# A two-layer hybrid encoder trunk: small products on all 128 rows of the TensorE array

## The chip, the cores and the metric

The kernel runs on one core of a Trainium2 chip. The core has five engines that run side by side, each through its own list of instructions in order: PE (TensorE, matrix products; the loading of its stationary operand has a row of its own, PEld), DVE (VectorE), ACT (ScalarE), POOL (GpSimd) and SP (SyncE, which here only issues DMAs). They meet through semaphores. PE reads SBUF and writes PSUM; DVE and ACT take its results from there. The metric is the device time of one execution in microseconds (us).

## The reference

528 tokens (16 meta tokens and a sequence of 512) of width 2048 pass two layers. The first has a convolution branch and a sparse attention branch, the second a gated linear recurrence of 16 heads. The parts that matter here:

```python
# layer 0, attention: scores of an indexer choose 128 keys for each query
dots = jnp.einsum('bqhd,bsd->bqhs', qi_b, ki)          # 16 heads of width 64, one set of keys
score = jnp.einsum('bqh,bqhs->bqs', wi_b, jax.nn.relu(dots))
score = jnp.where(admissible[None], score, NEG_INF)
_, idx = lax.top_k(score, topk)
...
p = jax.nn.softmax(logits, axis=-1)                    # 8 heads, bias by distance
return jnp.einsum('bhqk,bqkc->bqhc', p, c_sel)

# layer 1, one chunk of the recurrence
o_inter = jnp.einsum('bhtk,bhkv->bhtv', q_c * jnp.exp(b), state)
attn = jnp.einsum('bhtk,bhtsk,bhsk->bhts', q_c, jnp.exp(diff), k_c)
o_intra = jnp.einsum('bhts,bhsv->bhtv', attn, v_c)
state = jnp.exp(b_last)[..., None] * state \
        + jnp.einsum('bhsk,bhsv->bhkv', k_c * jnp.exp(b_last[:, :, None] - b), v_c)
```

Everything is float32. Around these stand the large projections (2048 to 2048 and wider), which are most of the arithmetic.

## The kernel before

Channels lie on the 128 partitions, tokens along the free dimension. Every large projection is cut into stripes of 128 output channels (`stripe`, L147). A stripe's weights come in two halves of 128x1024, each loaded by SP (L139), split by ACT into a rounded part `wh` (L143) and by DVE into the remainder `wl` (L144), with three buffers of each. PE then makes three products for each of 16 blocks of 128 input channels: L160 (`wh` by `xh`), L161 (`wh` by `xl`), L162 (`wl` by `xh`). These are the main products. A stripe over all 528 tokens has two sums of 264 columns, one over the 512 sequence tokens a single sum of 512. DVE evacuates the sums (L168).

The other products are side work. A scheduler sets the order on every engine while the program is built: work has a level (`band`), weights before evacuations, then side work, then the convolution on DVE (L415). The side products therefore stand among the main products of later stripes.

The first layer goes through the steps of `EVEN` (L46). `g` are stripes of the convolution branch, `s` those of the indexer, `k` the selection of keys on DVE (L389, L390), `h` an attention head, `n` a norm.

- `scores` (L356): one stripe gives two indexer heads, head A on partitions 0 to 63, head B on 64 to 127. Each head's queries are split into a rounded part and a remainder; the tile `qa` holds the rounded part on A's half and the remainder on the other half, which a DMA on POOL brings there (L367). The keys stand twice, on both halves, as `kih` (rounded) and `kil` (remainder). For each head and each of four query blocks PE makes a pair: L377, the whole tile by `kih`, on 128 rows of the array, and L378, the rounded queries by `kil`, on the 64 rows of that head. The fourth block is wider than 512 keys and has two pairs. ACT takes the relu (L380), DVE adds it to the score (L381).
- `attend` (L432): for each head and query block, POOL fetches the bias by DMA (L437) and adds the mask (L439), PE makes logits (L445), DVE and ACT the softmax, PE turns the probabilities (L463; L466 for the 16 meta keys) and multiplies them with the values (L470). The values `Vt` have five blocks of keys; block 0 is that of the 16 meta tokens, so the first product of each sum uses 16 rows. `Vt` has three buffers and is filled for two heads at a time (L334 to L344).

In the second layer `rec_head` (L639) makes the recurrence of one head out of small products. The state after the meta tokens is L751, a product on 16 rows; the later states are L754, and L757 and L758 make the output. `vt` (two buffers) holds the values, again with 16 meta tokens in block 0, and `kk` the turned keys, with those of the meta tokens in slot 3.

An f32 product such as L470 is run by PE as two MATMULs, so a line's count in the trace can be twice that of the code.

Of the kernel before, what the change touches and what calls it, by code (L numbers as in the profile page):

```python
# [10 lines left out]
F32 = mybir.dt.float32  # L11
F32R = mybir.dt.float32r
# [3 lines left out]
OP = mybir.AluOpType  # L16
# [54 lines left out]
def trunk_kernel(ctx: ExitStack, tc: tile.TileContext, x: bass.AP, w: bass.AP, wukv: bass.AP,  # L71
# [141 lines left out]
    def et(shape, dt, name, bufs):  # L213
        return epools[EROLE.get(name, "es")].tile(shape, dt, name=name, bufs=bufs)
# [50 lines left out]
    with band(SIDE):  # L265
        p = ps1()
        for t in range(NB):
            P.transpose(p[:, t * NM:(t + 1) * NM], kw[64:80, NM + 128 * t:NM + 128 * (t + 1)],
                        ident[64:80, 64:80])
        V.tensor_scalar(wiT.rearrange("p a b -> p (a b)"), p[:, :NB * NM], 1.0 / 32, None, op0=OP.mult)  # L270

        ki = et([128, T], F32, "gt", 3)
        G.dma_start(ki[:64], kw[:64])
        G.dma_start(ki[64:], kw[:64])
        kih, kil = split(epools["ei"], ki, 1.0, "kih", "kil", bufs=1)

# [40 lines left out]
    def keys_values(pr):  # L317
# [3 lines left out]
        for hh in range(2):  # L321
# [11 lines left out]
            Ks.append(Kh)  # L333
        Vs = [et([128, 5, 128], F32, "Vt", 3) for _ in range(2)]  # L334
        for i, (s0, ns) in enumerate(blocks):
            p = ps1()
# [19 lines left out]
    def scores(j):  # L356
# [6 lines left out]
        with band(EVAC):  # L363
            for q, hf, other in ((qa, lo, up), (qb, up, lo)):
                S.activation(q[hf], ps[0][0][hf], AF.Copy)
                V.tensor_tensor(ql[hf], ps[0][0][hf], q[hf].bitcast(F32), op=OP.subtract)
                G.dma_start(q[other], ql[hf])  # L367
        with band(SIDE):
            for t in range(NB):
                for hh in range(2):  # L370
                    h, W = 2 * j + hh, wk(t)
                    q, hf = ((qa, lo), (qb, up))[hh]
                    qs = slice(128 * t, 128 * (t + 1))
                    for s0, s1 in (((0, W),) if W <= 512 else ((0, HT), (HT, W))):
                        p = ps1()
                        se = max(s1, s0 + 256)
                        P.matmul(p[:, :se - s0], q[:, qs], kih[:, s0:se], start=True, stop=False)  # L377
                        P.matmul(p[:, :se - s0], q[hf, qs], kil[hf, s0:se], start=False, stop=True)  # L378
                        r = et([128, T], F32, "sq", 3)
# [52 lines left out]
    def attend(h, qh, gb, Kh, Vt):  # L432
# [24 lines left out]
        for t in range(NB):  # L457
# [4 lines left out]
            for j in range(t + 1):  # L462
                P.transpose(p[:, j * 128:(j + 1) * 128], L[:, NM + 128 * j:NM + 128 * (j + 1)], ident)  # L463
            S.activation(pt[:, 1:t + 2, :], p[:, :128 * (t + 1)], AF.Copy)
            p = ps1()
            P.transpose(p[:NM, :128], L[:, :NM], ident)  # L466
            S.activation(pt[:NM, 0, :], p[:NM, :128], AF.Copy)
            for j in range(t + 2):
                ns = blocks[j][1]
                P.matmul(o[:, 128 * t:128 * (t + 1)], Vt[:ns, j, :], pt[:ns, j, :],  # L470
                         start=j == 0, stop=j == t + 1)
# [167 lines left out]
    def rec_head(h, fz, q, v):  # L639
# [26 lines left out]
        S.activation(vt[:, 1:, :], p, AF.Copy, scale=1.0 / (KS * QS))  # L666
        p = ps1()
        P.transpose(p[:NM, :128], v[:, :NM], ident)
        S.activation(vt[:NM, 0, :], p[:NM, :128], AF.Copy, scale=1.0 / (KS * QS))
# [68 lines left out]
        for j in range(3):  # L738
            P.transpose(p[:, j * 128:(j + 1) * 128], kb[:, 128 * j:128 * (j + 1)], ident)
        P.transpose(p[:NM, 384:512], k[:, :NM], ident)  # L740
        kk = ht([128, 4, 128], F32, "kk", 2)
        S.activation(kk[:, :3, :], p[:, :384], AF.Copy, scale=KS * QS)
        S.activation(kk[:NM, 3, :], p[:NM, 384:512], AF.Copy, scale=KS * QS)
        o = pso()
        st = None
        for j in range(NB):
# [3 lines left out]
            if j == 0:  # L750
                P.matmul(p[:, :128], kk[:NM, 3, :], vt[:NM, 0, :], start=True, stop=True)  # L751
                V.tensor_copy(new, p[:, :128])
# [236 lines left out]
```

## Time and profile before

| | |
|---|---|
| median of 3 runs | 2024.43 us (2021.56 to 2024.53) |
| profiled execution | 2024.44 us |
| its span, first to last instruction | 2022.6 us |
| PE busy | 1995.4 us, 99% |
| PEld busy | 1814.4 us, 90% |
| DVE busy | 1298.9 us, 64% |
| ACT busy | 811.9 us, 40% |
| POOL busy | 88.8 us, 4% |
| chain that ended last | 95% PE |

The matmuls of PE are pipelined and their ends are modelled: one product's duration runs over into the next. The time that a product costs is the distance from its start to the start of the next. In the timeline a row gives the start and the length of one instruction, or of several alike in a row (x2, x6); the shape `64*128` means 64 rows by 128 columns of the array.

### The profile page before, as it was taken

To read this page: it belongs to the slowest core of one execution; us is meant where nothing else is said; L and a number is where in the kernel's file an instruction comes from. 1 tells how busy PE (TensorE), PEld (TensorE's weight loads), DVE (VectorE), ACT (ScalarE), POOL (GpSimd) and SP (SyncE) were. 2 spreads that over 40 slices of the span, in tenths; PEclk is the share of its full clock that TensorE was granted. 3 is DMA by queue.
4 is the path that set the end of the run, shared out by engine and by line. 5 is a ranking of instruction groups with operands and counts; after the bars stand their busy time and mean duration, and the time that the engine had idled before them with its cause. 6 is when DMAs were issued, how large, how long until landed. Compare 5 with 4: busy or idle time off the path is not lost.

```text
span 2022.6 us, 34969 instructions
## 1 busy us (share of the span) xinstructions
PE 1995.4 (99%) x14524; PEld 1814.4 (90%) x14524; DVE 1298.9 (64%) x2400; ACT 811.9 (40%) x1392; POOL 88.8 (4%) x121
## 2 busy tenths in 40 slices
PE   8999999999999999999999999999999999999997
PEld 7988779999999999999999999999999988888886
DVE  6588868997738545433577777777777773445334
ACT  5323343234343534322444555545555443224322
POOL 1000000011112100000000000000000000000000
PEclk9999999999999999999999999999999999999999
DMA  5422322233232233444222222222222222223333
GB/s 187 117 80 79 93 70 90 75 102 93 89 97 73 83 115 117 143 142 136 96 74 74 80 78 74 74 74 74 80 78 74 79 84 94 94 94 110 116 118 120
DMA packets 63279, 193.24 MB, mean 96 GB/s; under 512 B 7632, under 2 KB 12024, under 8 KB 63120
## 3 DMA queue, kind: packets, MB, share of 16 engines
q1 hardware_dynamic: 59168, 182.21, 28.0%
q0 software_dynamic: 3952, 8.80, 1.7%
q8 instruction: 114, 1.87, 0.4%
q14 instruction: 45, 0.37, 0.1%
HBM read 177.38 MB, written 11.22 MB: 93 GB/s over the span
## 4 chain that ended last, share of the span: by engine, by line
PE 95%; DVE 2%; ACT 1%; DMA 1%; issue 0%; SPq 0%; DVEq 0%; ACTq 0%
PE mps L162 27%; PE mps L161 27%; PE mps L160 27%; PE po L470 2%; PE s L378 1%; PE s L445 1%; PE s L377 1%; PE s L636 1%; PE s L635 1%; PE s L637 1%; PE po L758 1%; PE po L757 1%; PE s L341 1%; PE s L754 1%; PE s L330 1%; ACT xh L175 1%
## 5 line engine op out<-in xcount | busy, mean ns | idle before, releaser
L160 PE MATMUL mps<-xh,wh 128*128 128x264 f32 (+2 forms) x3728 | 1162.1, 312 | 10.0 <-ACT wh L143 3.3
L161 PE MATMUL mps<-xl,wh 128*128 128x264 f32 (+2 forms) x3728 | 1166.8, 313 | 2.1 <-DVE xl L176 2.0
L162 PE MATMUL mps<-xh,wl 128*128 128x264 f32 (+2 forms) x3728 | 1167.0, 313 | 1.7 <-DVE wl L144 1.5
L160 PEld LDWEIGHTS mps<-xh,wh 128*128 128x128 f32 (+1 forms) x3728 | 701.9, 188 | 52.5 <-ACT wh L143 4.0
L161 PEld LDWEIGHTS mps<-xl,wh 128*128 128x128 f32 (+1 forms) x3728 | 701.2, 188 | 47.1 <-DVE xl L176 4.5
L162 PEld LDWEIGHTS mps<-xh,wl 128*128 128x128 f32 (+1 forms) x3728 | 701.3, 188 | 43.5 <-DVE wl L144 2.8
L143 ACT ACTIVATE wh<-w 128x1024 fp32r<-128x1024 f32 (+1 forms) x293 | 310.2, 1059 | 675.6 <-PE mps L161 540.6
L144 DVE TENSOR_TENSOR wl<-w,wh 128x1024 fp32r<-128x1024 f32 (+1 forms) x293 | 361.1, 1233 | 249.7 <-ACT wh L143 247.6
L415 DVE SCALAR_TENSOR_TENSOR z<-u,vec,z 128x528 f32<-128x528 f32 x240 | 188.8, 796 | 2.8
L631 ACT ACTIVATE qhm<-q 128x256 f16<-128x256 f32 x128 | 52.1, 419 | 56.3 <-DVE q L732 44.2
L717 DVE COPY_PREDICATED A<-msk,s 128x256 f32<-128x256 uint8 x96 | 46.6, 485 | 28.3 <-PE s L637 27.7
L632 DVE SCALAR_TENSOR_TENSOR qlm<-q,qhm 128x256 f16<-128x256 f32 x128 | 53.1, 425 | 16.0 <-ACT qhm L631 16.0
L380 ACT ACTIVATE sq<-s 128x264 f32<-128x264 f32 (+3 forms) x80 | 31.3, 394 | 62.8 <-PE s L378 62.1
L168 DVE TENSOR_TENSOR gt<-mps,rstd 128x264 f32<-128x264 f32 x64 | 27.6, 431 | 39.3 <-PE mps L162 38.6
L381 DVE SCALAR_TENSOR_TENSOR mask<-sq,wiT,mask 128x264 f32<-128x264 f32 (+3 forms) x80 | 38.3, 494 | 22.3 <-ACT sq L380 21.9
L570 DVE TENSOR_TENSOR hin<-mps,hin 128x264 f32<-128x264 f32 x32 | 13.7, 432 | 48.2 <-PE mps L162 48.2
L631 ACT ACTIVATE kt1h<-k 128x256 f16<-128x256 f32 x64 | 26.6, 416 | 44.1 <-DVE k L723 44.1
L439 POOL TENSOR_TENSOR L<-L,mask 128x144 f32<-128x144 f32 (+3 forms) x32 | 36.1, 1128 | 162.7 <-DVE mask L392 88.2
L631 ACT ACTIVATE kt0h<-k 128x512 f16<-128x512 f32 (+1 forms) x64 | 33.3, 520 | 24.6 <-DVE k L723 24.2
L168 DVE TENSOR_TENSOR ta<-mps,rstd 128x512 f32<-128x512 f32 x16 | 11.1, 692 | 47.6 <-PE mps L162 47.6
L818 DVE TENSOR_TENSOR on<-mps,fz 128x512 f32<-128x512 f32 (+1 forms) x16 | 10.5, 658 | 48.3 <-PE mps L162 47.2
L723 DVE TENSOR_TENSOR k<-k,e 128x264 f32<-128x264 f32 (+1 forms) x96 | 40.9, 426 | 1.1
(301 smaller groups left out, 2085.9 us busy)
## 6 DMA issues: line engine op xcount, KB each, us to landing
w<-in_w_dram SPq DMA_DIRECT2D x293, 512.0 KB, 3.5
hin<-in_x_dram SPq DMA_DIRECT2D x16, 264.0 KB, 3.6
h1d<-hin SPq DMA_DIRECT2D x16, 264.0 KB, 2.1
fz<-h1d SPq DMA_DIRECT2D x15, 256.0 KB, 2.6
z<-in_x_dram SPq DMA_DIRECT2D x8, 264.0 KB, 5.8
L<-bdram POOLq DMA_DIRECT2D x8, 264.0 KB, 3.4
mbd<-mb SPq DMA_DIRECT2D x8, 264.0 KB, 2.8
mb<-mbd SPq DMA_DIRECT2D x8, 264.0 KB, 3.6
```

The lines of the kernel that those rows point to most:

```text
L143: S.activation(uh, used, AF.Copy)
L144: V.tensor_tensor(ul, used, uh.bitcast(F32), op=OP.subtract)
L160: P.matmul(o[:m], hi[:, ws], xh[:, sl], start=n == 0 and k == 0, stop=False)
L161: P.matmul(o[:m], hi[:, ws], xl[:, sl], start=False, stop=False)
L162: P.matmul(o[:m], lo[:, ws], xh[:, sl], start=False, stop=n == 1 and k == 7)
L168: V.tensor_tensor(dst[:, sl.start - o:sl.stop - o], p[:dst.shape[0]], rstd[:dst.shape[0], sl], op=OP.mult)
L415: eng.scalar_tensor_tensor(z, u[:, j:j + T], col(V_CW + i * CW + j), z, op0=OP.mult, op1=OP.add)
L470: P.matmul(o[:, 128 * t:128 * (t + 1)], Vt[:ns, j, :], pt[:ns, j, :], start=j == 0, stop=j == t + 1)
L631: S.activation(hi, src, AF.Copy, scale=scale)
L632: V.scalar_tensor_tensor(lo, src, scale, hi, op0=OP.mult, op1=OP.subtract)
L717: V.copy_predicated(A.rearrange("p b (n a m) -> p b n a m", a=2, m=mm)[:, :, :, 1, :], msk[:, li - 1 + i:li + i, :].rearrange("p b (n m) - ...
L723: V.tensor_tensor(klo, klo, eup.to_broadcast(list(klo.shape)), op=OP.mult)
```

## The change

Products on 64 or 16 rows become products on all 128, with zeros in one operand on the rows that are new.

- `kil` is no longer one tile with the remainder on both halves: the lower half has the remainder, the upper half is the keys less themselves, zero. L378 (L386 of the changed kernel) multiplies the whole query tile by it. For head B the rounded queries and the remainder therefore change places, so that the rounded ones lie on the lower half too.
- Block 0 of `Vt` and of `vt` is set to zero by POOL before the 16 rows of the meta tokens are written. L470 and L751 then run over 128 rows of it.
- The operands on the other side take whatever is in rows 16 to 127: the transposes L466 and L740 turn 128 columns instead of 16, and ACT copies all of it. In the recurrent head the two copies L742 and L743 become one.

```diff
-        kih, kil = split(epools["ei"], ki, 1.0, "kih", "kil", bufs=1)
+        kih = epools["ei"].tile([128, T], F32R, name="kih", bufs=1)
+        kil = epools["ei"].tile([128, T], F32R, name="kil", bufs=1)
+        S.activation(kih, ki, AF.Identity)
+        V.tensor_tensor(kil[:64], ki[:64], kih[:64].bitcast(F32), op=OP.subtract)
+        V.tensor_tensor(kil[64:], ki[64:], ki[64:], op=OP.subtract)
...
         Vs = [et([128, 5, 128], F32, "Vt", 3) for _ in range(2)]
+        for Vh in Vs:
+            G.memset(Vh[:, 0, :], 0.0)
...
-            for q, hf, other in ((qa, lo, up), (qb, up, lo)):
-                S.activation(q[hf], ps[0][0][hf], AF.Copy)
-                V.tensor_tensor(ql[hf], ps[0][0][hf], q[hf].bitcast(F32), op=OP.subtract)
+            for q, hi, lw, hf, other in ((qa, qa, ql, lo, up), (qb, ql, qb, up, lo)):
+                S.activation(hi[hf], ps[0][0][hf], AF.Copy)
+                V.tensor_tensor(lw[hf], ps[0][0][hf], hi[hf].bitcast(F32), op=OP.subtract)
                 G.dma_start(q[other], ql[hf])
...
                         P.matmul(p[:, :se - s0], q[:, qs], kih[:, s0:se], start=True, stop=False)
-                        P.matmul(p[:, :se - s0], q[hf, qs], kil[hf, s0:se], start=False, stop=True)
+                        P.matmul(p[:, :se - s0], q[:, qs], kil[:, s0:se], start=False, stop=True)
...
-            P.transpose(p[:NM, :128], L[:, :NM], ident)
-            S.activation(pt[:NM, 0, :], p[:NM, :128], AF.Copy)
+            P.transpose(p[:, :128], L[:, :128], ident)
+            S.activation(pt[:, 0, :], p[:, :128], AF.Copy)
             for j in range(t + 2):
-                ns = blocks[j][1]
-                P.matmul(o[:, 128 * t:128 * (t + 1)], Vt[:ns, j, :], pt[:ns, j, :],
+                P.matmul(o[:, 128 * t:128 * (t + 1)], Vt[:, j, :], pt[:, j, :],
                          start=j == 0, stop=j == t + 1)
...
+        G.memset(vt[:, 0, :], 0.0)
         P.transpose(p[:NM, :128], v[:, :NM], ident)
         S.activation(vt[:NM, 0, :], p[:NM, :128], AF.Copy, scale=1.0 / (KS * QS))
...
-        P.transpose(p[:NM, 384:512], k[:, :NM], ident)
+        P.transpose(p[:, 384:512], k[:, :128], ident)
         kk = ht([128, 4, 128], F32, "kk", 2)
-        S.activation(kk[:, :3, :], p[:, :384], AF.Copy, scale=KS * QS)
-        S.activation(kk[:NM, 3, :], p[:NM, 384:512], AF.Copy, scale=KS * QS)
+        S.activation(kk.rearrange("p a b -> p (a b)"), p, AF.Copy, scale=KS * QS)
...
-                P.matmul(p[:, :128], kk[:NM, 3, :], vt[:NM, 0, :], start=True, stop=True)
+                P.matmul(p[:, :128], kk[:, 3, :], vt[:, 0, :], start=True, stop=True)
```

The scheduler also sets some instructions at other places. On PE, in the first score stripe, before the change (`s_` and a number is a PSUM tile of side work, `mps` one of a stripe, `uh` here the tile of queries):

```order
L160 MATMUL mps<-xh,wh 128x264
L161 MATMUL mps<-xl,wh 128x264
L162 MATMUL mps<-xh,wl 128x264
L160 MATMUL mps<-xh,wh 128x264
L161 MATMUL mps<-xl,wh 128x264
L377 MATMUL s_1045<-kih,uh 128x256
L378 MATMUL s_1045<-kil,uh 128x256
L377 MATMUL s_1051<-kih,uh 128x272
L378 MATMUL s_1051<-kil,uh 128x272
L377 MATMUL s_1057<-kih,uh 128x272
L378 MATMUL s_1057<-kil,uh 128x272
L162 MATMUL mps<-xh,wl 128x264
```

And at the same place of the changed kernel, where L377 and L378 are L385 and L386:

```order
L160 MATMUL mps<-xh,wh 128x264
L161 MATMUL mps<-xl,wh 128x264
L385 MATMUL s_1046<-kih,uh 128x256
L386 MATMUL s_1046<-kil,uh 128x256
L385 MATMUL s_1052<-kih,uh 128x272
L386 MATMUL s_1052<-kil,uh 128x272
L385 MATMUL s_1058<-kih,uh 128x272
L386 MATMUL s_1058<-kil,uh 128x272
L162 MATMUL mps<-xh,wl 128x264
L160 MATMUL mps<-xh,wh 128x264
L161 MATMUL mps<-xl,wh 128x264
L162 MATMUL mps<-xh,wl 128x264
```

Three pairs stand three main products earlier; the pairs themselves are in the same order, and in the second layer the order on PE is unchanged.

On POOL, in the second attention head, before the change (`bdram` is the bias table, `L` a tile of logits; the brackets name the semaphores waited for):

```order
L439 TENSOR_TENSOR L<-L,mask_699 128x272 [waits DMASW0_49]
L437 DMA L<-bdram 128x1x400 [waits DMASW1_49,PE_49]
L439 TENSOR_TENSOR L<-L,mask_702 128x400 [waits DMASW1_49]
L437 DMA L<-bdram 128x1x528 [waits DMASW2_49,PE_49,Activation_49]
L439 TENSOR_TENSOR L<-L,mask_705 128x528 [waits DMASW2_49]
L437 DMA L<-bdram 16x1x16 [waits DMASW3_49,PE_49,Activation_49]
```

And at the same place of the changed kernel:

```order
L447 TENSOR_TENSOR L<-L,mask_700 128x272 [waits DMASW0_49]
L445 DMA L<-bdram 128x1x400 [waits DMASW1_49,PE_49]
L447 TENSOR_TENSOR L<-L,mask_703 128x400 [waits DMASW1_49]
L342 MEMSET Vt 128x128 [waits PE_49,Pool_49]
L445 DMA L<-bdram 128x1x528 [waits DMASW2_49,PE_49,Activation_49]
L447 TENSOR_TENSOR L<-L,mask_706 128x528 [waits DMASW2_49]
L445 DMA L<-bdram 16x1x16 [waits DMASW3_49,PE_49,Activation_49]
```

The memset of a `Vt` tile of a later head stands between the mask addition of the third query block and the bias DMA of the fourth, and waits for PE. The same holds in four later heads; the first three memsets stand at the start of the kernel, and the 16 of the second layer follow one another at the end of POOL's list.

## Rows read from the trace of the kernel before

**Rows 1.** The page: busy us (share of the span) and instructions of each engine.

```profile
PE 1995.4 (99%) x14524; PEld 1814.4 (90%) x14524; DVE 1298.9 (64%) x2400; ACT 811.9 (40%) x1392; POOL 88.8 (4%) x121
```

**Rows 2.** Waits of PE: who waited for whom, us in total, times, longest.

```profile
PE mps L160 <- DVE gt L168: 3.1, 4, 1.4
PE mps L160 <- ACT xh L175: 2.2, 1, 2.2
```

**Rows 3.** Timeline of PE, a score pair: start us, length, engine, line, operation.

```profile
185.90 0.28 PE L160 MATMUL mps<-xh,wh 128*128 128x264 f32 x1
186.02 0.28 PE L377 MATMUL s<-kih,uh 128*128 128x256 f32 x1
186.23 0.38 PE L378 MATMUL s<-kil,uh 64*128 64x256 f32 x1
186.54 0.39 PE L161 MATMUL mps<-xl,wh 128*128 128x264 f32 x1
186.76 0.28 PE L162 MATMUL mps<-xh,wl 128*128 128x264 f32 x1
```

**Rows 4.** Timeline of PE, two side products on 128 rows.

```profile
307.57 0.28 PE L330 MATMUL s<-ch,uh 128*128 128x264 f32 x1
307.69 0.28 PE L330 MATMUL s<-cl,uh 128*128 128x264 f32 x1
307.81 0.28 PE L160 MATMUL mps<-xh,wh 128*128 128x264 f32 x1
```

**Rows 5.** Timeline of PE, the products of one attention block.

```profile
503.44 0.28 PE L160 MATMUL mps<-xh,wh 128*128 128x264 f32 x1
503.66 1.35 PE L470 MATMUL po<-pt,Vt 16*128 16x128 f32 x8
...
504.97 0.28 PE L162 MATMUL mps<-xh,wl 128*128 128x264 f32 x1
```

**Rows 6.** Timeline of PE, four f32 instructions on 128 rows.

```profile
1081.48 0.28 PE L160 MATMUL mps<-xh,wh 128*128 128x264 f32 x1
1081.61 0.38 PE L757 MATMUL po<-q,st 128*128 128x128 f32 x2
1081.83 0.39 PE L758 MATMUL po<-A,vt 128*128 128x128 f32 x2
...
1082.17 0.29 PE L162 MATMUL mps<-xh,wl 128*128 128x264 f32 x1
```

**Rows 7.** Timeline of PE, the states of one recurrent head.

```profile
1112.82 0.40 PE L160 MATMUL mps<-xh,wh 128*128 128x512 f32 x1
1113.14 0.48 PE L751 MATMUL s<-vt,kk 16*128 16x128 f32 x2
1113.56 0.94 PE L754 MATMUL s<-vt,kk 128*128 128x128 f32 x6
...
1114.57 0.39 PE L162 MATMUL mps<-xh,wl 128*128 128x512 f32 x1
```

**Rows 8.** L378 alone: count, ns min/median/max, first and last start, shapes.

```profile
L378 PE MATMUL s<-kil,uh x40: 379/386/450, 103.3 to 292.2; 64*128 64x264 f32 x16, 64*128 64x256 f32 x8, 64*128 64x272 f32 x8, 64*128 64x400 f32 x8
```

**Rows 9.** Groups on POOL by shape: count, busy us, mean ns, idle before.

```profile
L352 POOL MEMSET mask<- 128x144 f32 x1 | 0.2, 218 | 0.3 <-POOLq L976 0.3
```

**Rows 10.** Timeline of POOL, the fourth block's bias in the second head.

```profile
437.79 0.52 POOL L437 DMA_DIRECT2D L<-bdram  x1 [7.22 <-ACT pt L467]
```

**Rows 11.** Windows: stretch, us, busy us of PE, PEld, DVE, ACT, POOL, clock, DMA.

```profile
103.00:117.00 14.00, 14.00 (x84) 11.05 (x83) 11.02 (x21) 5.45 (x12) 0.00 (x0) 1.00 0.25 76
307.00:455.00 148.00, 144.93 (x1144) 140.50 (x1144) 138.71 (x313) 41.69 (x80) 13.79 (x16) 1.00 0.29 91
```

**Rows 12.** The page's group of weight casts: busy us, mean ns, idle before.

```profile
L143 ACT ACTIVATE wh<-w 128x1024 fp32r<-128x1024 f32 (+1 forms) x293 | 310.2, 1059 | 675.6 <-PE mps L161 540.6
```

**Rows 13.** The page's group of weight loads of L160.

```profile
L160 PEld LDWEIGHTS mps<-xh,wh 128*128 128x128 f32 (+1 forms) x3728 | 701.9, 188 | 52.5 <-ACT wh L143 4.0
```

**Rows 14.** Windows: the stretch around PE's wait for an ACT cast.

```profile
786.00:800.00 14.00, 11.69 (x81) 11.27 (x81) 7.48 (x12) 6.52 (x11) 0.00 (x0) 0.88 0.25 80
```

More of the change, by code (lines that the diff above doesn't have):

```diff
@@ L371, in scores @@
                     h, W = 2 * j + hh, wk(t)
-                    q, hf = ((qa, lo), (qb, up))[hh]
+                    q = (qa, qb)[hh]
                     qs = slice(128 * t, 128 * (t + 1))
```

## The prediction

> **What bounds the kernel.** I read the busy times first: PE is busy for 1995.4 us of a span of 2022.6 us [rows 1]. A busy PE is not yet PE at its peak, so I went on to the waits. The two that matter here are 3.1 us on a DVE evacuation of a sum (four times) and 2.2 us on an ACT cast [rows 2]. Between them PE works through its list, so the time is the sum of the spacings at which PE starts its products, and every change is priced in spacings. These are read from the timeline of PE as the difference of start times; the durations of single products overlap and are of no use for a sum.
>
> Main products of 264 columns (L160 to L162) follow each other every 0.12 us. The score pair among them does not fit that rhythm [rows 3]. From the start of the L160 before it (185.90) to the second main product after it (L162 at 186.76) 0.86 us go by, for four products: L160, L377, L378 and L161. At 0.12 each they would take 0.48. The 0.38 too many lie where L378 stands, which uses 64 rows of the array: 0.21 before it starts, 0.31 until the next 128-row product, and 0.22 more until the one after that. That the score product alone is not the cause is seen in the next stretch [rows 4]: two side products on 128 rows (L330), set between main products in the same way, and the main product behind them start at 307.57, 307.69 and 307.81, 0.12 apart.
>
> The 16-row products show the same. L470 at 503.66 stands for four products of f32 data, which PE runs as eight instructions, the first two on 16 rows. From the L160 before (503.44) to the second main product after (504.97) it is 1.53 us [rows 5]. On 128 rows an f32 instruction of 128 columns takes 0.11: four of them and two main products take 0.69 (1081.48 to 1082.17) [rows 6], thus 4 x 0.11 + 2 x 0.12. For the sum of L470 that makes 8 x 0.11 + 2 x 0.12 = 1.12 and an excess of 0.41, or 0.39 with 0.112 for one (0.69 less 0.24, by four). In the recurrent heads the L751 pair and six L754 take 1.75 us from 1112.82 to 1114.57 [rows 7], with main products of 512 columns at 0.23 on both sides: 8 x 0.112 + 2 x 0.23 = 1.36, an excess of 0.39. So **one visit to fewer rows costs 0.38 to 0.41 us**, whether it is one product or two instructions, 64 rows or 16. I take 0.39.
>
> **The change part by part.** It widens L378, the first product of each L470 sum, and L751.
> - Scores: 8 stripes, with 2 heads and 5 pairs each (the widest of the four query blocks is cut in two), thus 80 visits; the trace has them as two groups of 40 [rows 8]. 80 x 0.39 = 31.2 us.
> - Attention: 8 heads x 4 blocks = 32 visits, 12.5 us.
> - Recurrent heads: 16 visits, 6.2 us.
> - Together 128 visits, 49.9 us. The products L476 and L480, the small ones of the meta tokens, stay on 16 rows and keep their cost.
>
> What the widened products cost is bounded by the nearest rows on both sides. At best they stream like the 128-row products beside them, 0.12 and 0.11 [rows 4, 6]; below that there is nothing to be had, since the number of columns stays. At worst they keep the excess. I take the first, because the L330 pair shows the same data type on the same kind of side work with the same neighbours.
>
> What is added: 24 memsets of 128x128 on POOL. The nearest row is one of 128x144 at 0.218 us [rows 9], so some 5 us in all on an engine that is idle nearly always. One of them stands on POOL between the mask addition for one query block and the bias DMA for the next. It waits for the last product that read the old V tile; behind it is the bias DMA, and behind that the softmax of the next block. In the run before, POOL stood idle for 7.22 us at just this place [rows 10], and 0.2 us fit in. If that cover were gone, each later bias would delay its block's transposes on PE by as much. The memsets of the recurrent heads stand alone on POOL; the ACT copy of 16 rows that now waits for them fills a tile that was last read two heads earlier. On DVE the low part of the keys becomes two operations instead of one, under 1 us more; L378 reads it first at 103.3 us [rows 8], long after it is written. One ACT copy per recurrent head merges with its neighbour. The wider transposes have the same moving columns. All these I cost at nothing.
>
> What is late next: DVE. In the score part of a stripe (103 to 117 us) it is busy for 11.02 of 14 us [rows 11]. Ten visits less make that part about 10.1 us, so DVE has 0.9 us more work than time there and falls behind. What covers it: the casts of weights run ahead of PE, since ACT is idle for 540.6 us before them until PE frees a buffer [rows 12], and the rest of each stripe has room to catch up. I cost this at nothing, but it is the first rival. In the selection of the top keys (307 to 455 us) DVE is busy for 138.71 of 148 us and PE for only 144.93 [rows 11], so PE already waits there. The seven visits that go in this stretch, 2.7 us, I count as lost: PE would only wait longer.
>
> The sum is 49.9 - 2.7 = 47.2 us. It is made against the profiled execution, 2024.44 us with a span of 2022.6, which equals the median of 2024.43. 2024.4 - 47.2 = **1977 us**. With 0.40 a visit and nothing lost it is 1973; with 0.38, and the 3.1 us of waits on DVE doubled, 2024.4 - 48.6 + 2.7 + 3.1 = 1982. Its own range is 1972 to 1983.
>
> **The rivals.**
> 1. DVE sets the pace of the score part and the selection. For it: 138.71 of 148 and the 11.02 against 10.1 above. Against it: in the score part PE is busy for 14.00 of 14 us [rows 11], so nothing has been late there yet. If half of the scores' 31.2 us and all of the 2.7 go: 2024.4 - 49.9 + 15.6 + 2.7 = 1993. If all of the 31.2 go, 2008.
> 2. The loads of the widened products are no longer hidden. If a load on the same rows could not run beside a product, the 80 + 64 + 32 = 176 widened instructions would each show a load of 0.188 us [rows 13]: 33.1 us given back, 2024.4 - 49.9 + 33.1 = 2008. Against it: the main products load for 0.188 and still follow each other every 0.12 on the same rows. The Trainium skill has such a rule ("TensorE: Matmul & The Clock Gate", Part 3, The mechanism): a load overlaps running products "only when row_grp differs", that is, on other row groups. The trace disagrees with it here: the change of rows is where the spacing is long.
> 3. The change doesn't do what it says: the excess hangs on something other than the row count, such as the operands that were written by DMA. Then the visits stay, and it is 2024. Against it: three kinds of product with different operands show one excess, and L377, which reads the same weights' tile on 128 rows, is followed by the gap and not preceded by it.
> 4. Slower: with the visits gone PE reaches the places at which DVE is late, stops, and its clock drops. The run before has one such stop, the 2.2 us on an ACT cast [rows 2], and the granted clock over the 14 us around it is 0.88 of 2.4 GHz on the mean [rows 14], so 1.7 us more are lost in a stretch at the lower level, 1.2 GHz. A stop thus costs 3.9 us, and from 13 stops on the gain of 49.9 is gone. One in each of the 8 score stripes and at each of the 7 visits of the selection are 15: 2024.4 - 49.9 + 58.5 = 2033. Against it: the longest of the four stops in the selection was 1.4 us [rows 2], and the clock stayed at 1.00 there [rows 11].
>
> **How the numbers follow.** The forecast gets 0.73, rival 1 gets 0.18 (half of it below 1996), rivals 2, 3 and 4 get 0.03 each. The range of 1971 to 1996 holds the forecast, with 1 us below its best sum, and the nearer half of rival 1: 0.82. Faster by over 0.2%, which is about what a measurement of this kernel can tell from no change, are the forecast and rivals 1 and 2, 0.94; no change is rival 3, 0.03; slower is rival 4, 0.03.
>
> **What would show it.** In the changed kernel's timeline the score pair between main products should take 0.48 us where it took 0.86, the four-product group of L470 1.14 instead of 1.53, and the eight instructions in the recurrent heads 1.36 instead of 1.75. The stretch from the first to the last score product should be some 31 us shorter, and each recurrent head 0.39. The forecast is wrong if these spacings stay, if PE's waits for DVE grow by over 10 us, or if a POOL memset ends just before an ACT copy or a bias DMA that PE then waits for.

## The result, and the profile after

| | before | after |
|---|---|---|
| median | 2023.46 us (4 runs, 2021.56 to 2024.53) | 1974.41 us (4 runs, 1972.42 to 1975.23) |
| profiled execution | 2024.44 us | 1972.42 us |
| its span | 2022.6 us | 1970.3 us |

The ratio is 0.9757, with a 95% interval of 0.974 to 0.9774: faster, by 49 us. The forecast was 1977 us, with a range of 1971 to 1996. One execution each of two later kernels ran at a mean granted clock of 0.556 and took some 3180 us; the medians below are those of the others.

The busy times of the changed kernel, to be set beside [rows 1]:

```profile
PE 1944.1 (99%) x14524; PEld 1803.8 (92%) x14524; DVE 1293.6 (66%) x2401; ACT 805.5 (41%) x1376; POOL 93.9 (5%) x145
```

PE makes the same 14524 instructions and is still busy for 99% of the span. It is busy for 51.3 us less, and the span is 52.3 us shorter. No other engine has become the bound. The loads are as many as before, but they now fill 92% of the span.

PE's waits, which answer to [rows 2]:

```profile
PE mps L160 <- DVE gt L168: 3.1, 4, 1.4
...
PE mps L160 <- ACT xh L175: 1.2, 1, 1.2
```

The four waits for DVE are the same to the tenth of a microsecond. The wait for the ACT cast is 1.0 us shorter. Around it the clock held in this execution, where it was 0.88 before [rows 14]. The columns of this window are those of [rows 11]; the third from the end is the granted clock:

```profile
739.00:753.00 14.00, 12.69 (x102) 12.27 (x101) 10.76 (x16) 7.69 (x14) 0.00 (x0) 1.00 0.23 77
```

PE's timeline at a score pair, where L377 and L378 are now L385 and L386 [rows 3]:

```profile
185.83 0.28 PE L160 MATMUL mps<-xh,wh 128*128 128x264 f32 x1
185.95 0.28 PE L385 MATMUL s<-kih,uh 128*128 128x264 f32 x1
186.07 0.28 PE L386 MATMUL s<-kil,uh 128*128 128x264 f32 x1
186.19 0.29 PE L161 MATMUL mps<-xl,wh 128*128 128x264 f32 x1
186.31 0.29 PE L162 MATMUL mps<-xh,wl 128*128 128x264 f32 x1
```

From the L160 before the pair to the second main product behind it 0.48 us go by, where it was 0.86. Every start is 0.12 behind the one before. The next view has one attention group [rows 5] and the states of one recurrent head [rows 7]:

```profile
468.19 0.28 PE L160 MATMUL mps<-xh,wh 128*128 128x264 f32 x1
468.31 1.05 PE L478 MATMUL po<-pt,Vt 128*128 128x128 f32 x8
469.12 0.37 PE L161 MATMUL mps<-xl,wh 128*128 128x264 f32 x1
469.33 0.28 PE L162 MATMUL mps<-xh,wl 128*128 128x264 f32 x1
...
1107.74 0.39 PE L160 MATMUL mps<-xh,wh 128*128 128x512 f32 x1
1107.97 0.38 PE L759 MATMUL s<-vt,kk 128*128 128x128 f32 x2
1108.19 0.83 PE L762 MATMUL s<-vt,kk 128*128 128x128 f32 x6
1108.78 0.47 PE L161 MATMUL mps<-xl,wh 128*128 128x512 f32 x1
1109.09 0.40 PE L162 MATMUL mps<-xh,wl 128*128 128x512 f32 x1
```

They take 1.14 us (1.53 before) and 1.35 us (1.75 before). The single L386 [rows 8] and its weight load (count, ns min/median/max, first and last start):

```profile
L386 PEld LDWEIGHTS s<-kil,uh x40: 187/188/192, 102.9 to 264.3; 128*128 128x128 f32 x40
L386 PE MATMUL s<-kil,uh x40: 277/285/348, 103.0 to 264.4; 128*128 128x264 f32 x16, 128*128 128x256 f32 x8, 128*128 128x272 f32 x8, 128*128 128x400 f32 x8
```

The load of 128 rows takes 188 ns and is hidden, since the products follow each other at 0.12.

The two profiled spans cut at the same products show where the time came from:

| stretch | before | after | less |
|---|---|---|---|
| first to last score product (start to start) | 203.57 | 172.40 | 31.17 |
| last score product to the last product of the attention (end to end) | 439.76 | 427.51 | 12.25 |
| from there to the first state product of the recurrence | 282.35 | 279.71 | 2.64 |
| first to last state product (L751, L759) | 630.91 | 625.28 | 5.63 |
| all the rest | 466.0 | 465.4 | 0.6 |

The first, second and fourth row are the visits. The third, 2.64 us, has none in it: the shorter wait for the cast and the clock that held make it up, 1.0 and, by the prediction's figure, 1.7 us. These two are no effect of the visits. The wait ends with the landing of one DMA (`mb` from `mbd`), which took 5.20 us before and 4.20 after. A later kernel (the one on 96 rows, below) has the same order on PE and none of the 128 visits, but its trace has 4.91 us for that DMA, a wait of 1.9 us, and this clock in the same window:

```profile
739.00:753.00 14.00, 12.10 (x85) 11.69 (x85) 9.86 (x15) 8.44 (x15) 0.00 (x0) 0.88 0.26 80
```

From the attention to the first state product that trace has 2.0 us more than the changed kernel's. The profiled execution of the changed kernel is the fastest of its four, and that of the kernel before is 1 us above its median: the two spans lie 52.3 us apart and the medians 49.1.

### The profile page after: what moved, and what is told of

Its sections match the earlier page's. It is cut to its first block, busy times and chain, and to the rows that moved or that the text cites. A ratio compares the mean times of both kernels' runs of the same rounds, so it can differ in the third digit from the quotient of the medians.

```text
span 1970.3 us, 35020 instructions
## 1 busy us (share of the span) xinstructions
PE 1944.1 (99%) x14524; PEld 1803.8 (92%) x14524; DVE 1293.6 (66%) x2401; ACT 805.5 (41%) x1376; POOL 93.9 (5%) x145
## 4 chain that ended last, share of the span: by engine, by line
PE 95%; DVE 3%; ACT 1%; DMA 0%; issue 0%; SPq 0%; DVEq 0%; ACTq 0%
PE mps L162 27%; PE mps L161 27%; PE mps L160 27%; PE po L478 1%; PE s L453 1%; PE s L644 1%; PE s L643 1%; PE s L645 1%; PE po L766 1%; PE po L765 1%; PE s L349 1%; PE s L336 1%; PE s L762 1%; PE s L386 1%; PE s L385 1%; ACT xh L175 0%
## 5 line engine op out<-in xcount | busy, mean ns | idle before, releaser
L160 PE MATMUL mps<-xh,wh 128*128 128x264 f32 (+2 forms) x3728 | 1160.3, 312 | 9.1 <-ACT wh L143 3.4
L160 PEld LDWEIGHTS mps<-xh,wh 128*128 128x128 f32 (+1 forms) x3728 | 701.3, 188 | 49.4 <-ACT wh L143 4.1
L143 ACT ACTIVATE wh<-w 128x1024 fp32r<-128x1024 f32 (+1 forms) x293 | 309.7, 1057 | 659.5 <-PE mps L161 534.2
L639 ACT ACTIVATE kt0h<-k 128x512 f16<-128x512 f32 (+1 forms) x64 | 33.2, 518 | 24.9 <-DVE k L732 24.4
L751 ACT ACTIVATE kk<-s 128x512 f32<-128x512 f32 x16 | 9.6, 600 | 81.2 <-PE s L749 81.2
L741 DVE TENSOR_TENSOR q<-q,e 128x256 f32<-128x256 f32 x96 | 40.5, 422 | 1.6
```

What stands on the lines that cost most here:

```text
L143: S.activation(uh, used, AF.Copy)
L160: P.matmul(o[:m], hi[:, ws], xh[:, sl], start=n == 0 and k == 0, stop=False)
L639: S.activation(hi, src, AF.Copy, scale=scale)
L741: V.tensor_tensor(qup, qup, halves(e[:, eo:], 1)[0].to_broadcast([128, n, m]), op=OP.mult)
```

## The experiments

My theory: **one visit of PE to a smaller part of the array costs a fixed 0.39 us, and nothing else in the change has a price.** The rivals are that the time came from another order or another part of the change, that the price hangs on each product or on the number of rows left out, and that some visits cost nothing. Each median below is to be set against the 1974.41 us of the changed kernel; the kernel before, measured again beside them, took 2023.44 to 2024.60 us where it had 2023.46. "Price" means what is left of the distance from the main product before a visit to the second product behind it, after the nominal spacings (0.12 for 264 columns, 0.11 for 128 in f32) are taken off, summed over the whole trace.

### Undoing one part at a time

Scores back on 64 rows (with them the old split of keys and queries; `...` marks what is left out):

```diff
+kih, kil = split(epools["ei"], ki, 1.0, "kih", "kil", bufs=1)
...
-P.matmul(p[:, :se - s0], q[:, qs], kil[:, s0:se], start=False, stop=True)
+P.matmul(p[:, :se - s0], q[hf, qs], kil[hf, s0:se], start=False, stop=True)
```

> The changed kernel with its 80 second score products back on 64 rows (and with them the split of kil and of q as it was before); the attention and the recurrence stay on 128 rows. Theory (a price of 0.39 us for each visit to fewer rows): 80 visits, 31 us more than the 1974.4 us of the changed kernel, so about 2005.5 us; a pair takes 0.86 us from the last main product before it to the first behind it, and first to last score product takes 203 us as before the change, against 172. Rival (the 31 us between the two kernels came from another part of the change or from another order of the main products, and the row count is no cause): 1974 to 1980 us, with the pair near 0.48 us.

Attention's first product back on 16 rows:

```diff
+ns = 128 if j else 16
-P.matmul(o[:, 128 * t:128 * (t + 1)], Vt[:, j, :], pt[:, j, :],
+P.matmul(o[:, 128 * t:128 * (t + 1)], Vt[:ns, j, :], pt[:ns, j, :],
```

> The changed kernel with only the first product of each attention block (32 of them) back on 16 rows. Theory (0.39 us a visit, all of it on the path): 32 x 0.39 = 12.5 us more, about 1987 us; the group of that line takes 0.39 us longer. Rival, which the prediction held for the seven visits in the selection of the best keys: DVE paces that stretch, so that seven of the visits cost nothing: 25 x 0.39 = 9.8 us, about 1984 us, and PE's waits for DVE there get shorter by 2.7 us in sum. Rival (row count no cause): 1974 us.

The recurrence's first product back on 16 rows:

```diff
-P.matmul(p[:, :128], kk[:, 3, :], vt[:, 0, :], start=True, stop=True)
+P.matmul(p[:, :128], kk[:16, 3, :], vt[:16, 0, :], start=True, stop=True)
```

> The changed kernel with only the first state product of each recurrent head (16 of them) back on 16 rows. Theory (0.39 us a visit): 16 x 0.39 = 6.2 us more, about 1980.6 us, and from the first to the last of these products 15 x 0.39 = 5.9 us more than the 625.3 us of the changed kernel. Rival (the heads wait on another engine, and PE has the time to spare): 1974 to 1976 us, with shorter waits of PE in the recurrence.

| put back | visits | median | ratio to before, interval | above 1974.41 | price in the trace | each |
|---|---|---|---|---|---|---|
| scores | 80 | 2005.81 | 0.9908, 0.9894 to 0.9923 | 31.4 | 31.9, against 0.15 | 0.397 |
| attention | 32 | 1986.96 | 0.9819, 0.9802 to 0.9835 | 12.6 | 12.86, against 0.54 | 0.385 |
| recurrence | 16 | 1980.48 | 0.9783, 0.9768 to 0.9797 | 6.1 | 6.23, against -0.06 | 0.393 |
| all three | 128 | 2023.46 (before) | | 49.1 | | |

The intervals are some 3 us to either side, so it is the trace that gives the third decimal. The three alone add up to 50.0 us, and the whole change was worth 49.1: within the intervals the parts don't interact. First to last score product is 203.56 us again. With the attention put back, the stretch behind the scores takes 439.85 us, as before the change. PE's waits for DVE are 3.1 us, 4, 1.4 in this kernel too. So the rival of that run, by which seven visits are free, falls. In the recurrence the stretch from the first to the last state product grew by 5.5 us, where I had expected 5.9.

The order on PE is no cause either. The kernels with the attention and the recurrence put back have the same order of products on PE as the changed kernel (by the tiles that the trace names), and so do those on 96 and 64 rows below. The kernel with the 64-row scores does get the order of before back, all of it, so that its time alone doesn't separate the two; its trace does, since the prices read at the 80 visits (31.9 us) fill the 31.2 us by which the stretch is longer. The wider transposes and the memsets are no cause: the kernel with the attention put back keeps them and has the old stretch.

What PE and its loads do at a visit is seen in the kernel with the 64-row scores. First the products, then the weight loads (PEld) of the same moment, both start and length:

```profile
185.88 0.28 PE L160 MATMUL mps<-xh,wh 128*128 128x264 f32 x1
186.00 0.28 PE L381 MATMUL s<-kih,uh 128*128 128x256 f32 x1
186.21 0.38 PE L382 MATMUL s<-kil,uh 64*128 64x256 f32 x1
186.52 0.39 PE L161 MATMUL mps<-xl,wh 128*128 128x264 f32 x1
186.75 0.28 PE L162 MATMUL mps<-xh,wl 128*128 128x264 f32 x1
```

```profile
185.88 0.19 PEld L381 LDWEIGHTS s<-kih,uh 128*128 128x128 f32 x1
186.21 0.18 PEld L382 LDWEIGHTS s<-kil,uh 64*128 64x128 f32 x1
186.51 0.19 PEld L161 LDWEIGHTS mps<-xl,wh 128*128 128x128 f32 x1
186.62 0.19 PEld L162 LDWEIGHTS mps<-xh,wl 128*128 128x128 f32 x1
```

A load between products on 128 rows starts with the product ahead of it: L381's starts at 185.88, with the L160, 0.12 before L381 itself. The load of the 64-row product does not. It starts at 186.21, 0.21 after the product ahead. The load back to 128 rows (186.51) comes 0.30 after the product on 64 rows. So two loads a visit don't start with the product ahead of them. They take 0.183 and 0.188 us on the mean, together 0.37 of the 0.39. That was the next theory to test.

### One price for a visit or for a product

The 64-row products in twos: both wide products first, then the two narrow ones, held together by an order on PE (shortened here). In one kernel the two are those of heads A and B, on different halves of the rows; in the other they are of one head.

```diff
+for hh, t, s0, s1 in pieces:                       # a visit's two pieces
+    wide = P.matmul(p[:, :se - s0], q[:, qs], kih[:, s0:se], start=True, stop=False)
+for (hh, t, s0, s1), (p, q, qs, se) in zip(pieces, got):
+    hf = (lo, up)[hh]
+    with tc.issue_after(wide.ins):
+        P.matmul(p[:, :se - s0], q[hf, qs], kil[hf, s0:se], start=False, stop=True)
```

> The changed kernel with its 80 second score products back on 64 rows, but ordered in twos: the two products on 128 rows of the two heads of a pair first, then their two products on 64 rows one behind the other, one on rows 0 to 63 and one on rows 64 to 127 (40 visits of two instead of 80 of one). Theory A (the price is one for each visit, 0.39 us, for the two weight loads at its ends that stream no columns): 40 x 0.39 = 15.7 us above 1974.4 us, about 1990 us. Rival B (the price is one for each product on fewer rows): 80 x 0.39 = 31 us, about 2006 us, as with the 80 visits. Rival C (a load inside a visit is hidden in part only; two products on 16 rows in one visit had 0.10 us beside the price of the visit): 40 x 0.49 = 19.6 us, about 1994 us. Rival D (products on different halves of the rows run beside each other): 1990 us less 40 x 0.11 = 1986 us.

> As the kernel in twos, but both products of a visit are of one head and so on the same 64 rows: 32 visits of two and 16 of one, 48 in all. Theory A (a price for each visit): 48 x 0.39 = 18.8 us above 1974.4 us, about 1993 us. Rival B (a price for each product): about 2006 us. Rival C (0.10 us for the second load of a visit): 18.8 + 32 x 0.10 = 22.0 us, about 1996 us. Rival D (a load is beside the product ahead of it only where the two are on different rows, as the Trainium skill has it in TensorE: Matmul & The Clock Gate, Part 3, The mechanism): the second load of a visit is not hidden either, 18.8 + 32 x 0.19 = 24.9 us, about 1999 us, while the visits on two halves stay at 1990 us or below.

On different halves: 1983.80 us (ratio to before 0.9802, 0.9788 to 0.9817), a price of 10.9 us over 40 visits, 0.27 each. On one half: 1991.94 us (0.9841, 0.9826 to 0.9855), 18.9 us over 48 visits, 0.395 each. A visit with two products on one half thus costs what a visit with one does (theory A of that run; rival C would have made 22.0 us of it, D 24.9). On different halves it costs 0.12 less than that, which is one product's spacing: D of that run. D expected 1986 us; the price in the trace makes 1985.3 of it, and the median is 1.5 us below that. Timeline of PE and of its loads for two halves:

```profile
183.84 0.28 PE L380 MATMUL s<-kih,uh 128*128 128x256 f32 x1
184.04 0.39 PE L385 MATMUL s<-kil,uh 64*128 64x256 f32 x2
184.35 0.52 PE L380 MATMUL s<-kih,uh 128*128 128x272 f32 x2
```

```profile
184.04 0.19 PEld L385 LDWEIGHTS s<-kil,uh 64*128 64x128 f32 x2
```

And for one half:

```profile
183.26 0.40 PE L380 MATMUL s<-kih,uh 128*128 128x256 f32 x2
183.59 0.51 PE L385 MATMUL s<-kil,uh 64*128 64x256 f32 x2
184.03 0.39 PE L161 MATMUL mps<-xl,wh 128*128 128x264 f32 x1
```

```profile
183.59 0.30 PEld L385 LDWEIGHTS s<-kil,uh 64*128 64x128 f32 x2
```

On two halves the two loads together take 0.19, as long as one of them, and the two products 0.39, as long as one: they run side by side. On one half the two loads take 0.30, so the second begins 0.11 after the first and is hidden behind the product on the same rows. The Trainium skill ("TensorE: Matmul & The Clock Gate", Part 3, The mechanism) says that products at different tile positions run together. The trace agrees, with 0.39 us for two. The same section says that a load runs beside products only where the row groups differ, though a sentence above it also lets a load into the background weight buffer go ahead. With the "only" the trace does not agree: loads on one half, and on 128 rows, are hidden as well.

### How many rows, and how long the load

The attention product of the second experiment, with 96 and with 64 rows in place of 16.

```diff
-ns = 128 if j else 16
+ns = 128 if j else 96        # and 64
```

> The changed kernel with only the first product of each attention block (32 of them) on 96 rows, 80 of them zeros. Theory A (what counts is that the array is set to another number of rows, and 96 rows need the whole array as 128 do): nothing, about 1974 us. Rival B (any row count that differs from the neighbours' costs a visit): 32 x 0.39 = 12.3 us more, about 1987 us, as on 16 rows.

> The changed kernel with only the first product of each attention block (32 of them) on 64 rows, 48 of them zeros. Theory A (the price is that of a change of the array's rows, whatever their number): 32 x 0.39 = 12.3 us more, about 1987 us, as on 16 rows. Rival B (the price grows with the rows that are left out, 112 of 128 on 16 rows): half of it, 7 us, about 1981 us.

96 rows: 1975.2 us (0.9758, 0.9742 to 0.9774), and a price of 0.57 us over 32 products against 0.54 on 128 rows. 64 rows: 1987.75 us (0.982, 0.9804 to 0.9837) and 12.9 us. The line alone, PE, first on 96 and then on 64 rows, shows it in the longest duration:

```profile
L479 PE MATMUL po<-pt,Vt x224: 272/275/276, 304.8 to 699.7; 128*128 128x128 f32 x80, 96*128 96x128 f32 x32
```

```profile
L479 PE MATMUL po<-pt,Vt x224: 271/276/378, 304.5 to 711.7; 128*128 128x128 f32 x80, 64*128 64x128 f32 x32
```

So the price doesn't grow with the rows that are left out: 16 and 64 cost the same, 96 nothing. The zeros need not have filled all 128 rows.

For the load, the changed kernel has eight visits that are cheaper: L484, the transposes of 16x16, 0.29 us each. Their own load has 16 columns. It is given 128 (and the bias rows are fetched 128 wide for it, which is left out here):

```diff
...
-P.transpose(p[:NM, :NM], L[:NM, :NM], ident[:NM, :NM])
+P.transpose(p[:, :NM], L[:NM, :128], ident[:NM, :NM])
```

> The changed kernel with its eight transposes of 16 rows given a weight of 128 columns instead of 16 (112 of the 128 output rows are not used). In the changed kernel these eight visits cost 0.29 us each, where the others cost 0.39, and their own weight loads take 82 ns, where those of 128 columns on fewer rows take 183. Theory (the price of a visit is the two weight loads at its ends, which stream no columns beside them): with loads of 183 ns the price rises by 0.10 us to 0.39 us, so by 0.8 us over the eight. Rival (the array takes a fixed time to change its rows, and these visits are cheap for the few columns that they stream): 0.29 us as now.

The load of that line in the changed kernel, and in this one:

```profile
L484 PEld LDWEIGHTS s<-ident,L x8: 81/82/83, 393.3 to 699.7; 16*16 16x16 f32 x8
```

```profile
L484 PEld LDWEIGHTS s<-ident,L x8: 133/134/135, 393.8 to 700.6; 16*128 16x128 f32 x8
```

The load got 52 ns longer, not the 101 that I had expected, and the distance from the transpose to the next product grew from 109 to 160 ns (medians of eight), by 51. In this step the price follows the load one for one; a fixed price falls. The visit is now 0.34 us, and the loads at its two ends 0.134 + 0.188 = 0.32. For the three kinds of visit (loads of 82, 134 and 183 ns) the price is the two loads and 0.02 us. That is as far as it is shown: why a load starts late when the shape changes, the records don't tell. The median of one run is 1972.74 us, which can't show 0.4 us.

### A version that beats both

The 16 leading positions of the attention, which the change left on 16 rows, on 128:

```diff
-L = softmax(None, NM, 0, NM)
+L = softmax(None, 128, 0, NM, load=128)
...
-P.transpose(p[:NM, :NM], L[:NM, :NM], ident[:NM, :NM])
+P.transpose(p[:, :128], L[:, :128], ident)
...
-P.matmul(p[:, :NM], Vt[:NM, 0, :], pt[:NM, 0, :NM], start=True, stop=True)
+P.matmul(p[:, :NM], Vt[:, 0, :], pt[:, 0, :NM], start=True, stop=True)
```

> The changed kernel with the two products that it left on 16 rows, the transpose and the value product of the 16 leading positions of each attention head, made on 128 rows as well (8 of each; the probabilities are worked out for 128 queries instead of 16). Theory (0.39 us a visit): 16 x 0.39 = 6.2 us less, about 1968 us, on one side. Rival (a visit is dear only where main products stand close on both sides; these two stand where PE waits for the head's probabilities): 1973 to 1975 us. Rival (the wider probabilities, 128x16 instead of 16x16 on ACT and DVE and a 64 KB bias load instead of 1 KB, come later than the narrow ones, and PE waits for them): above 1975 us, with a wait of PE ahead of that transpose.

> The kernel with the 16 leading positions of the attention made on 128 rows as well, once more, beside the version built on it. By the first measurement 1967.8 us; by the trace of its first run 4.7 us less than the changed kernel in the attention, so between 1967 and 1970 us.

1967.76 us (ratio to before 0.972, interval 0.9706 to 0.9735), and 1967.44 us in the second measurement (0.9722, 0.9709 to 0.9736). The medians are 6.7 and 7.0 us below the changed kernel, near the 6.2 expected, but the visits give less. From the product ahead of a visit to the second one behind it, the eight value products (L488) gained 0.29 us each. The eight transposes (L484) gained 0.19 and not 0.29: 0.545 us became 0.352, which is the spacing of a wide transpose and two main products. The edit also widens the weights of the eight logit products L453 from 16 to 128 columns, and they gained 0.12 each. Together that is 4.8 us, and the stretch from the scores to the end of the attention is 4.6 us shorter in both.

The 2 us between are not in these visits. The traces show where they can come from. PE's wait for the ACT cast is 0.6 to 0.7 us in all five traces of kernels that fetch these bias rows 128 wide, with the full clock behind it. It is 1.2 to 2.2 us in the other nine, and in four of those the lower clock follows. In the kernel on 96 rows this made 2.0 us against the profiled execution of the changed kernel, the fastest of its four. Why the wait is shorter here, no run tells. PE's waits don't grow in sum.

On top of that, the last visits ahead of the scores were widened, four transposes to 80 rows and three bias products to 128:

```diff
-P.transpose(p[:, t * NM:(t + 1) * NM], kw[64:80, NM + 128 * t:NM + 128 * (t + 1)], ident[64:80, 64:80])
+P.transpose(p[:, t * 80:(t + 1) * 80], kw[:80, NM + 128 * t:NM + 128 * (t + 1)], ident[:80, :80])
...
-P.matmul(p[:HB, :352], rt, oh[:32, :352], start=True, stop=True)
+P.matmul(p[:HB, :352], rt, oh[:, :352], start=True, stop=True)
```

> The kernel with the 16 leading positions of the attention made on 128 rows as well, and with the last visits ahead of the scores gone: the four transposes of the key weights on 80 rows instead of 16 (one visit), and the three products of the bias table on 128 rows with zeros in 96 (three visits; POOL fills the zeros). Theory: 0.39 us for the one and 0.29 us for each of the three, whose weights have 8 columns: 1.3 us less than the kernel that it is built on, 1966.5 us by the 1967.8 us measured for that one. Rival (96 rows are free, but 80 rows are not): 0.9 us less. Rival (the zeros come late, and the bias table with them; PE waits at the first attention products): slower than 1968 us, with a wait of PE for DVE or ACT before 300 us.

1967.7 us (0.9723, 0.971 to 0.9737): nothing that can be measured against 1967.44, and not the 1.3 us less. The transposes gained 0.22 us. The bias products gained nothing:

```profile
47.05 0.28 PE L160 MATMUL s<-xh,wh 128*128 128x264 f32 x1
47.26 0.76 PE L312 MATMUL s<-z,rt 128*8 128x352 f32 x2
47.95 0.39 PE L161 MATMUL s<-xl,wh 128*128 128x264 f32 x1
48.18 0.28 PE L162 MATMUL s<-xh,wl 128*128 128x264 f32 x1
```

On 128 rows, but with weights of 8 columns, L312 starts 0.21 after the product ahead, just as a visit does. So a visit is not a matter of rows alone, and my theory was too narrow. The last run widens the columns as well:

```diff
-rt = et([128, HB], F32, "rt", 1)
+rt = et([128, T], F32, "z", 8)                    # 128 columns, zeros from the ninth on
-P.matmul(p[:HB, :352], rt, oh[:, :352], start=True, stop=True)
+P.matmul(p[:, :352], rt[:, :128], oh[:, :352], start=True, stop=True)
```

> The version that makes the bias products on 128 rows, with their weight widened from 8 to 128 columns as well (zeros in 120 of them; the output rows behind the eighth are not used). On 128 rows and 8 columns these three products still cost their visit: 0.21 us to the first instruction of the pair and 0.39 us from the second to the next main product, as on 32 rows. Theory (a weight of 8 columns sets the array to another shape just as 32 rows do, so both have to be full): the first start comes 0.12 us behind the main product ahead of it, and the price of 0.29 us a visit goes, 0.9 us over the three. Rival (columns are no cause; two instructions of 352 columns in 4-byte numbers cost this on any shape): 0.21 and 0.39 us as they are.

```profile
46.22 0.28 PE L160 MATMUL s<-xh,wh 128*128 128x264 f32 x1
46.34 0.75 PE L312 MATMUL s<-z 128*128 128x352 f32 x2
46.66 0.55 PE L161 MATMUL s<-xl,wh 128*128 128x264 f32 x1
47.06 0.28 PE L162 MATMUL s<-xh,wl 128*128 128x264 f32 x1
```

From the L160 before to the second product behind 0.84 us go by instead of 1.13: the price of 0.29 is gone, with the load now at 188 ns instead of 88. The one run took 1965.62 us, the lowest of all, but one run is no measurement against 1967.44: the stretch ahead of the scores took 101.6 us in it, and between 102.9 and 104.9 us in the other traces.

## Why the prediction was right

- **PE's spacings are the time.** It held. PE's busy time fell by 51.3 us and the span by 52.3, in the two profiled executions.
- **A visit costs 0.39 us, whatever it holds.** It held for the three kinds that the change removes: 0.397, 0.385 and 0.393 over the whole traces, each part put back by itself. It doesn't hold for all: a short load makes it 0.29, two halves 0.27. What I had as "fewer rows" is less exact too: 96 rows are free, and 8 columns cost as 32 rows do.
- **Scores 31.2, attention 12.5, recurrence 6.2.** Measured 31.4, 12.6 and 6.1 by the medians of the runs that put them back, with some 3 us to either side.
- **The widened products stream like their neighbours.** They did, at 0.12 and 0.11 us. Rival 2, a load of 0.188 shown by each of 176 instructions, falls.
- **2.7 us lost in the selection, because "PE would only wait longer".** This step failed, and the forecast of 1977 instead of 1974.5 (2024.4 less 49.9) is its size. PE waited for DVE for 3.1 us before and for 3.1 us after. I had read a queue into two busy shares (138.71 of 148 us for DVE [rows 11]). The four waits are not a backlog that a faster PE lengthens. In the trace each ends with an evacuation that had to let DVE finish what it was at: in three of them one operation of 0.7 us of the selection (L397 or L398, which were L389 and L390), in the fourth two, of 0.76 and 0.48 us. None of the visits stands at these four places. The count was off as well: the trace before has six visits from 307 to 455 us, and the next starts at 455.5. That 1974.5 lies 0.1 us from the median is partly luck, since the executions of this kernel differ by up to 2.8 us.
- **DVE falls behind in the score part (rival 1, 0.18).** It did not. DVE is busy for 159.47 of the 172.68 us of the scores, 92%, and PE for all of them. The casts still run ahead: the page after has ACT idle for 534.2 us before L143 until PE is done with a buffer, 540.6 before [rows 12]. In the first stripe DVE has 12.72 of 14 us where it had 11.02, and PE 14.00 as before.
- **Stops that lower the clock (rival 4).** None was added. The one that there was got shorter, and this gave the 2.64 us that nobody had forecast for that stretch. The visits are not the reason: that wait is 0.6 to 2.2 us over the fourteen traces, and the granted clock fell to its lower level behind it in four of them, that of the kernel on 96 rows among them.
- **The change does what it says (rival 3).** The excess went with the widened products and came back with each of them, in the attention and the recurrence with nothing else on PE changed.
- **The memsets on POOL cost nothing.** 24 of 0.20 to 0.22 us, and the trace names nobody who waited for one.

## What to carry to other kernels

Where small products stand among full ones, look at PE's start-to-start distances and at the load ahead of each product: a load that starts late, and not with the product ahead, marks a change of the array's shape, which cost 0.27 to 0.39 us here for leaving and coming back. Pad the operands with zeros until the shape is that of the neighbours (96 rows were enough here, and columns count too), or put several narrow products into one visit. A busy share of 94% on another engine is no proof that time saved on PE is lost: look at what ends each single wait.

## What the runs showed of the hardware that I had not expected

- A product on 96 rows costs as one on 128 (0.57 against 0.54 us over 32 products), one on 64 as one on 16 (12.9 against 12.86).
- Two products on different halves of the rows ran side by side: the two took 0.39 us together, and 40 visits were 0.12 us cheaper each.
- Few weight columns can cost as few rows do, but not always. L312 in f32 with 8 columns pays 0.29 us. L349 of the changed kernel, with 16 columns between products of 128, pays nothing, neither on the way in nor on the way out (timeline, every start 0.11 to 0.12 behind the last):

```profile
442.98 0.28 PE L336 MATMUL s<-ch,ul 128*128 128x264 f32 x1
443.10 0.28 PE L349 MATMUL s<-uh,ch 128*16 128x256 f32 x1
443.21 0.28 PE L349 MATMUL s<-uh,cl 128*16 128x256 f32 x1
...
443.68 0.28 PE L349 MATMUL s<-ul,ch 128*16 128x256 f32 x1
443.79 0.28 PE L349 MATMUL s<-uh,ch 128*128 128x256 f32 x1
```

L349 uses the rounded type, with one MATMUL for each product, and L312 the full f32 with two. The number of columns is not the difference: L453 of the changed kernel, full f32 in two MATMULs with 16 columns, starts late as L312 does, 0.21 us behind the product ahead, and got 0.12 us cheaper with 128 columns:

```profile
383.66 0.27 PE L475 MATMUL s<-ident,L 128*128 128x128 f32 x1
383.87 0.21 PE L453 MATMUL s<-Kh,qh 128*16 128x16 f32 x2
384.01 0.39 PE L161 MATMUL mps<-xl,wh 128*128 128x264 f32 x1
```

The transposes L466 of the kernel before, 16 columns in one MATMUL each, start 0.11 us behind the product ahead and cost nothing, so widening them gained nothing. Whether it is the two MATMULs that make the difference, no run here separates from the rest.
